# A hybrid decoder trunk: sparse-attention projections in three wide chunks with a borrowed accumulator, and a new order of the early steps

## The chip, the cores and the metric

The kernel runs on one core of one Trainium2 chip, in one launch. The metric is the device time of an execution in microseconds (us), taken as the median of several runs. Engines are called by their names in the profile: PE is TensorE's matmul side and PEld its weight loads, DVE is VectorE, ACT is ScalarE, POOL is GpSimd, SP is SyncE, on whose queue most DMAs are issued.

## The reference

Two layers of a decoder trunk, sequence 512, model width 1024, all in float32. Per layer one projection feeds four parallel branches, which are lifted, gated, summed and projected out; a SwiGLU feed-forward follows.

```python
h = rmsnorm(x, norm_mix)
(a_x, a_b, a_c, d_q, d_k, d_v, i_q, i_k, i_w,
 g_q, g_f, g_i, g_g, m_q, gate_logits) = split_cols(h @ w_in)
y_a = a_b * causal_conv3(a_c * a_x, conv_w)                        # A: gated convolution
q = partial_rope(rmsnorm(d_q ...8 heads of 64...), cos, sin)       # B: sparse attention
k = partial_rope(rmsnorm(d_k ...1 head...), cos, sin)
iq = partial_rope(i_q ...8 heads of 64...); ik = partial_rope(i_k); iw = i_w * 8 ** -0.5
y_b = dsa_attention(q, k, d_v, iq, ik, iw)   # score = sum_h relu(iq . ik / 8) * iw; the best 128 keys
                                             # of each query; softmax attention over those
y_c = ...hgrn2 gated linear recurrence of g_q, g_f, g_i, g_g...    # C
y_m = ...cross attention of m_q into 256 memory tokens, 4 heads of 128...   # M
merged = sum over n of sigmoid(gate_logits)[n] * (branches[n] @ w_lift[n])
x = x + merged @ w_out
gate, up = split(rmsnorm(x, norm_ffn) @ ffn_w_up)
x = x + (silu(gate) * up) @ ffn_w_down
```

## The kernel before

**Products in three passes.** Every large product is done in split float32: a high and a low part of each operand, and three matmuls per tile (`mm3`, lines 270 to 272). The parts of a weight chunk are made on the chip: `Chunk` loads up to 2048 columns per partition into `w_raw` (two buffers, issued on SP), then ACT writes `w_hi` (`A`, line 97) and DVE `w_lo` (line 225), 1024 columns at a time, three buffers each.

**Accumulators.** PSUM holds three buffers "mm" (`mm_ps`, for products), two "at" (`at_ps`, for attention logits and outputs) and three "tr" (`tr_ps`, for transposes and small results). A buffer comes free when the engines that read it are done, in the order in which the program asked for buffers.

**Who sets the order.** The program is recorded step by step, and a scheduler lays the instructions of each engine into a fixed order; each engine then runs its own list strictly in turn. Splits of weights and some evictions are recorded with a priority 3000 places ahead (`AHEAD`). Steps are Python generators, and a string gives the order in which they are advanced. For the early part of each layer that is `EARLY[l]`: "b" is a step of `projections` (sparse attention), "c" of `conv_branch`, "m" of `mem_branch`, "s" of `sel`, the chain of `select(1)`, `select(2)`, `select(3)`. What is left of b, c and m after the string is run out; what is left of `sel` is woven into `lift(3)`.

**The steps.**
- `projections`: five chunks of 256, 256, 200, 256 and 256 columns. For each, the four tiles of 128 tokens follow one another: `tokens` makes one accumulator (8 k x 3 matmuls, h stationary and the weights moving), and a handler works it off at once: `c_kv`, `c_iq`, `c_last` and `c_q`. Handlers copy heads out (`unit`, `twin`), norm and rotate them (`headnorm`, `rope`), and transpose them (`heads_T`, line 754; `twin`, line 776) into qS, kS, iqS and ikS.
- `mem_branch`: a head pair is projected, then four steps per pair, each a chain: logits into an at buffer (`mk`, `qg`), maximum on DVE (line 639), exponential on ACT (`mprob`), scaling on DVE (line 651), four transposes (line 653), copies to `mpt_hi` (ACT) and `mpt_lo` (DVE, line 657), output product into the other at buffer, copies to y_m. `mpt_hi` and `mpt_lo` have one buffer each. Two of the products stand in "m" steps of their own, eight attention steps in eight more.
- `select(t)`: 8 heads of index scores in at buffers (lines 685, 686), summed on DVE, then 16 rounds of `max` and `match_replace` on DVE, giving the bias of query tile t.
- `lift(n)`: gates and lift products in pairs of 128 columns, woven with `sel` (for n = 3) or with `attend` (for n = 0, followed by `values`).
- `attend(t)`: 8 heads: logits in at buffers, line 698 on DVE, exponential and scaling on ACT (`prob`), transposes (line 709), copies `pt` on ACT, products with vt (line 715). Then the HGRN stage begins with `logits`, whose results zf, zq and zg (line 880) lie in space that the attention used.
- `final`, at the very end of the kernel, already has a product that opens all four token tiles at once on three mm buffers and one at buffer, with `tokens_wide`: for each part of the weights, for each of the four tiles, all k of that part.

Of the kernel before, what the change touches and what calls it, by code (L numbers as in the profile page):

```python
# [16 lines left out]
AF = mybir.ActivationFunctionType  # L17
# [4 lines left out]
P = 128  # L22
S = 512
NT = S // P
D = 1024
KD = D // P
# [11 lines left out]
C_AX, C_AB, C_AC, C_DQ, C_DK, C_IQ, C_IK = 0, 512, 1024, 1536, 2048, 2176, 2688  # L38
# [3 lines left out]
NONC = -2.0e38  # L42
OFF = -1.0e30
AHEAD = 3000
EARLY = ["mmbcmmbmmbsccsmmcsssmsccbmb", "mmbmmbmmcbsccsmmcsssmsccbmb"]
MM_BUFS = 3
TR_BUFS = 3
AT_BUFS = 2
# [21 lines left out]
def hybrid_trunk(ctx: ExitStack, tc: tile.TileContext, x, mem, positions, norm_mix, w_in, conv_w,  # L70
# [19 lines left out]
    def A(dst, src, func, **kw):  # L90
        name = tables.get(func)
        if name is not None and name != table["set"]:
            load = act.preload_act_table_set(name)
            for u in table["users"]:
                tc.add_manual_dep(load.ins, u.name, order, reason="table set")
            table.update(set=name, load=load.ins, users=[])
        i = act.activation(dst, src, func, **kw)  # L97
        if name is not None:
            tc.add_manual_dep(i.ins, table["load"].name, order, reason="table set")
            table["users"].append(i.ins)  # L100
        return i

    def mm_ps():
        return pmm.tile([P, 512], F32, name="mm")

    def at_ps():
        return pat.tile([P, 512], F32, name="at", bufs=AT_BUFS)

    def tr_ps():
        return pat.tile([P, 512], F32, name="tr", bufs=TR_BUFS)  # L110
# [31 lines left out]
    ps = tr_ps()  # L142
# [16 lines left out]
    ps = tr_ps()  # L159
# [19 lines left out]
    gq_b, gk_b = [], []  # L179
    for l in range(DEPTH):  # L180
        a = sp.tile([P, HD], F32, name=f"gq_raw{l}")
# [5 lines left out]
        b = consts.tile([P, HD], F32, name=f"gk{l}")  # L187
# [64 lines left out]
    def tokens(w, a, t, ps, k0=0, kt=None):  # L252
        kt = w.kt if kt is None else kt
        for k in range(k0, k0 + w.kt):
            mm3(ps, pair(a, k, slice(t * P, (t + 1) * P)), w.at(k - k0), k == 0, k == kt - 1)

    def tokens_wide(ws, a, kt, pss):

        k0 = 0
        for w in ws:  # L260
            for ks, _, _ in w.parts:
                for t, ps in enumerate(pss):
                    for k in ks:
                        mm3(ps, pair(a, k0 + k, slice(t * P, (t + 1) * P)), w.at(k), k0 + k == 0, k0 + k == kt - 1)
            k0 += w.kt

    def mm3(ps, a, b, first, last):
        ah, al = a
# [105 lines left out]
    h = new_h()  # L374
# [126 lines left out]
    def mixer(l, h, norms, cm, cf):  # L501
        mix = cm.enter_context(tc.tile_pool(name="mix", bufs=1, side="right"))
        r_t, r_b = norms()
        r8_t = small(NT, name="r8_t", bufs=2)
# [171 lines left out]
        with pool_("dsa") as dp:  # L676
            qS = dp.tile([P, 8, S], F32R, name="qS")
            kS = (dp.tile([P, S], F32R, name="k_hi"), dp.tile([P, S], F32R, name="k_lo"))
            pool.memset(f(kS[1][HD:P, :]), 0.0)
            vt = dp.tile([P, NT, HD], F32, name="vt")  # L680
# [42 lines left out]
            with pool_("idx") as ip:  # L723
                iqS = ip.tile([P, 8, S], F32R, name="iqS")
                ikS = (ip.tile([P, S], F32R, name="ik_hi"), ip.tile([P, S], F32R, name="ik_lo"))
                pool.memset(f(ikS[1][HD:P, :]), 0.0)
                iw = ip.tile([P, NT, 8], F32, name="iw")

                def rope(u, heads, t):
                    v = u[:, :, 0:ROT]  # L730
                    c = cos2[:, t:t + 1, :].to_broadcast([P, heads, ROT])
                    s = sin2[:, t:t + 1, :].to_broadcast([P, heads, ROT])
                    a = ip.tile([P, 4, ROT], F32, name="rope_a", bufs=2)[:, :heads]
                    b = ip.tile([P, 4, ROT], F32, name="rope_b", bufs=2)[:, :heads]
                    dve.tensor_mul(a, v, c)
                    dve.tensor_mul(b, v, s)
                    hf = ROT // 2
                    dve.tensor_sub(v[:, :, 0:hf], a[:, :, 0:hf], b[:, :, hf:])
                    dve.tensor_add(v[:, :, hf:], a[:, :, hf:], b[:, :, 0:hf])

                def headnorm(u, heads, gain):
                    sq = ip.tile([P, 4, HD], F32, name="hn_sq", bufs=1)[:, :heads]
                    A(sq, u, AF.Square, scale=HD ** -0.5)
                    ms = small(heads)
                    dve.tensor_reduce(ms, sq, axis=AX.X, op=OP.add)
                    r = small(heads)
                    rstd_into(r, ms, small, heads)
                    dve.tensor_mul(u, u, r[:, :, None].to_broadcast([P, heads, HD]))
                    dve.tensor_mul(u, u, gain[:, None, :].to_broadcast([P, heads, HD]))

                def heads_T(dst, h0, u, heads, t):
                    ps = tr_ps()[:, :heads * HD]
                    for i in range(heads // 2):
                        pe.transpose(ps[:, i * P:(i + 1) * P], u[:, i * P:(i + 1) * P], ident)  # L754
# [12 lines left out]

                def twin(ps, t, c0, norm, dst):
                    u = ip.tile([P, 2, HD], F32, name="twin", bufs=2)
                    A(u[:, 0, :], ps[:, c0:c0 + HD], AF.Copy, scale=r_t[:, t:t + 1])  # L770
                    if norm:
                        headnorm(u[:, 0:1], 1, gk_b[l])
                    rope(u[:, 0:1], 1, t)
                    dve.tensor_copy(u[:, 1, :], u[:, 0, :])
                    ps = tr_ps()[:, :P]
                    pe.transpose(ps, u.rearrange("p a b -> p (a b)"), ident)
                    s = slice(t * P, (t + 1) * P)
                    A(dst[0][:, s], ps, AF.Copy)
                    dve.tensor_sub(dst[1][0:HD, s], ps[0:HD], f(dst[0][0:HD, s]))

                def iq_part(ps, t, c0, heads, h0):
                    u = unit(ps, t, c0, heads)
                    rope(u, heads, t)
                    heads_T(iqS, h0, u.rearrange("p a b -> p (a b)"), heads, t)

                def c_kv(ps, t):
                    A(vt[:, t, :], ps[:, 64:128], AF.Copy, scale=r_t[:, t:t + 1])
                    twin(ps, t, 0, True, kS)
                    iq_part(ps, t, 128, 2, 0)

                def c_iq(ps, t):
                    iq_part(ps, t, 0, 4, 2)

                def c_last(ps, t):
                    A(iw[:, t, :], ps[:, 192:200], AF.Copy, scale=r8_t[:, t:t + 1])
                    iq_part(ps, t, 0, 2, 6)
                    twin(ps, t, 128, False, ikS)

                def c_q(q):
                    def go(ps, t):  # L800
                        u = unit(ps, t, 0, 4)
                        headnorm(u, 4, gq_b[l])
                        rope(u, 4, t)
                        heads_T(qS, 4 * q, u.rearrange("p a b -> p (a b)"), 4, t)
                    return go

                def select(t):
                    n = (t + 1) * P
# [307 lines left out]
```

## Time and profile before

| | before |
|---|---|
| three runs | 2047.5, 2048.2, 2047.55 us |
| median | 2047.55 us |
| the profiled execution, its own time | 2047.48 us |
| its span, first to last instruction | 2045.4 us |
| mean granted TensorE clock | 0.999 |
| DMA traffic | 203.79 MB, mean 100 GB/s |

The span is 2.1 us shorter than the execution's own time, which also holds what lies around the first and the last instruction. In rows of the timeline, the first number is the start in us from the span's start, the second the duration; in tables of stretches, each engine's busy time comes with its count of instructions, then the granted clock, the DMA share and GB/s. In lists of waits the three numbers are us in total, times, and the longest. Rows of the timeline that are alike and follow one another are merged and carry their count.

### The profile page before, as it was taken

The page shows a single profiled execution, that of the slowest core. Times are in us where ns is not written, and L with a number is a line of the kernel's source. Part 1 is how long each engine was busy: PE and PEld are TensorE (multiplying, and loading weights), DVE is VectorE, ACT ScalarE, POOL GpSimd, SP SyncE. Part 2 cuts the span into 40 slices and gives each one's busy share as a digit, 9 for nine tenths or more (in the row PEclk, how much of TensorE's full clock was granted, in tenths as well). Part 3 has the DMA queues.
Part 4 walks back from the last instruction along what each step waited for, and adds up shares of the span by engine and source line. Part 5 has one row for each costly group of instructions (what it writes and reads, how often), then busy time and mean ns, then how long its engine had stood idle before and what let it go on. Part 6 is the DMA issues. An engine that isn't in the chain of part 4 may idle for free.

```text
span 2045.4 us, 26581 instructions
## 1 busy us (share of the span) xinstructions
PE 2034.5 (99%) x10348; PEld 1715.8 (84%) x10348; DVE 1269.3 (62%) x2507; ACT 1017.5 (50%) x1834; POOL 9.8 (0%) x33
## 2 busy tenths in 40 slices
PE   8999999999999999999999999999999999999999
PEld 8998988888888888888889898888888888888887
DVE  6779998547676544334457889963777754533442
ACT  7653655766665423223355456576767633322331
POOL 0000000000000000000000000000000000000000
PEclk9999999999999999999999999999999999999999
DMA  7632232223233232233243213322223322323322
GB/s 253 220 89 94 68 93 93 64 71 93 78 118 113 83 103 93 93 105 102 87 155 94 88 58 107 97 76 63 83 83 101 126 90 96 103 75 111 97 79 93
DMA packets 187709, 203.79 MB, mean 100 GB/s; under 512 B 4270, under 2 KB 176384, under 8 KB 187456
## 3 DMA queue, kind: packets, MB, share of 16 engines
q1 hardware_dynamic: 183872, 193.56, 29.8%
q10 hardware_dynamic: 3552, 8.41, 1.1%
q8 instruction: 81, 1.33, 0.3%
q14 instruction: 44, 0.36, 0.1%
q0 software_dynamic: 160, 0.13, 0.0%
HBM read 191.60 MB, written 10.49 MB: 99 GB/s over the span
## 4 chain that ended last, share of the span: by engine, by line
PE 99%; DMA 1%; DVE 0%; ACT 0%; SPq 0%; issue 0%; DVEq 0%
PE mm L270 30%; PE mm L272 30%; PE mm L271 30%; PE tr L715 1%; PE tr L709 1%; PE at L686 1%; PE at L685 1%; PE at L272 1%; PE at L270 1%; PE at L271 1%; DMA w_raw<-in_mem_w_kv_dram 1%; PE at L963 0%; PE at L937 0%; PE tr L653 0%; PE tr L754 0%; PE tr L972 0%
## 5 line engine op out<-in xcount | busy, mean ns | idle before, releaser
L270 PE MATMUL mm<-h_hi,w_hi 128*128 128x512 f32 x1664 | 653.0, 393 | 0.0
L271 PE MATMUL mm<-h_lo,w_hi 128*128 128x512 f32 x1664 | 652.1, 392 | 0.0
L272 PE MATMUL mm<-h_hi,w_lo 128*128 128x512 f32 x1664 | 650.1, 392 | 0.0
L225 DVE TENSOR_TENSOR w_lo<-w_raw,w_hi 128x1024 fp32r<-128x1024 f32 (+1 forms) x346 | 419.5, 1213 | 364.5 <-ACT w_hi L97 361.3
L97 ACT ACTIVATE w_hi<-w_raw 128x1024 fp32r<-128x1024 f32 (+1 forms) x346 | 363.4, 1051 | 460.8 <-PE mm L271 414.5
L272 PEld LDWEIGHTS mm<-h_hi,w_lo 128*128 128x128 f32 x1664 | 312.8, 188 | 64.8 <-issue 1.2
L270 PEld LDWEIGHTS mm<-h_hi,w_hi 128*128 128x128 f32 x1664 | 312.8, 188 | 64.5 <-issue 2.2
L271 PEld LDWEIGHTS mm<-h_lo,w_hi 128*128 128x128 f32 x1664 | 312.9, 188 | 63.8 <-issue 2.0
L272 PE MATMUL mm<-w_hi,h_lo 128*128 128x256 f32 (+1 forms) x448 | 128.2, 286 | 0.0
L271 PE MATMUL mm<-w_lo,h_hi 128*128 128x256 f32 (+1 forms) x448 | 127.0, 285 | 0.0
L270 PE MATMUL mm<-w_hi,h_hi 128*128 128x256 f32 (+1 forms) x448 | 127.0, 285 | 0.0
L271 PE MATMUL mm<-a_lo,w_hi 128*128 128x512 f32 x272 | 106.3, 391 | 0.0
L270 PE MATMUL mm<-a_hi,w_hi 128*128 128x512 f32 x272 | 106.0, 390 | 0.0
L272 PE MATMUL mm<-a_hi,w_lo 128*128 128x512 f32 x272 | 105.8, 391 | 0.0
L270 PE MATMUL mm<-y_hi,w_hi 128*128 128x512 f32 x256 | 101.4, 397 | 0.0
L272 PE MATMUL mm<-y_hi,w_lo 128*128 128x512 f32 x256 | 100.6, 393 | 0.0
L271 PE MATMUL mm<-y_lo,w_hi 128*128 128x512 f32 x256 | 100.3, 392 | 0.0
L272 PEld LDWEIGHTS mm<-w_hi,h_lo 128*128 128x128 f32 x448 | 85.8, 191 | 1.4 <-issue 0.8
L270 PEld LDWEIGHTS mm<-w_hi,h_hi 128*128 128x128 f32 x448 | 85.3, 191 | 1.2 <-issue 0.8
L271 PEld LDWEIGHTS mm<-w_lo,h_hi 128*128 128x128 f32 x448 | 85.6, 191 | 0.6
L97 ACT ACTIVATE a_hi<-fg 128x512 fp32r<-128x512 f32 x44 | 27.8, 633 | 109.4 <-DVE fg L1065 109.4
L97 ACT ACTIVATE prob<-prob,small 128x128 f32<-128x128 f32 (+3 forms) x128 | 69.2, 554 | 15.2 <-DVE small L698 14.6
(358 smaller groups left out, 2946.9 us busy)
## 6 DMA issues: line engine op xcount, KB each, us to landing
w_raw<-in_w_in_dram SPq DMA_DIRECT2D x72, 1024.0 KB, 5.3
w_raw<-in_ffn_w_up_dram SPq DMA_DIRECT2D x44, 1024.0 KB, 5.1
w_raw<-in_w_lift_dram SPq DMA_DIRECT2D x32, 512.0 KB, 3.5
w_raw<-in_ffn_w_down_dram SPq DMA_DIRECT2D x16, 1024.0 KB, 5.5
w_raw<-in_mem_w_kv_dram SPq DMA_DIRECT2D x8, 1024.0 KB, 5.4
w_raw<-in_w_out_dram SPq DMA_DIRECT2D x8, 1024.0 KB, 5.2
w_raw<-in_ffn_w_down_dram SPq DMA_DIRECT2D x10, 512.0 KB, 3.4
kv<-kv ACTq DMA_DIRECT2D x8, 512.0 KB, 3.2
```

Source lines behind the costliest of these rows:

```text
L97: i = act.activation(dst, src, func, **kw)
L225: dve.tensor_sub(lo, raw[:, k:e], f(hi))
L270: pe.matmul(ps, ah, bh, start=first, stop=False)
L271: pe.matmul(ps, ah, bl, start=False, stop=False)
L272: pe.matmul(ps, al, bh, start=False, stop=last)
L685: pe.matmul(ps, q[:, hh, s], k[0][:, :n], start=True, stop=False)
L686: pe.matmul(ps, q[:, hh, s], k[1][:, :n], start=False, stop=True)
L709: pe.transpose(pp[:, (2 * e + i) * P:(2 * e + i + 1) * P], probs[2 * i + e][:, b * P:(b + 1) * P], ident)
L715: pe.matmul(pv[e * HD:(e + 1) * HD, :], vt[:, b, :], pt[:, b, e * 2 * P:(e + 1) * 2 * P], start=b == 0, stop=b == t)
```

## The change

The five chunks become three: 512 columns (query heads 6 and 7, the key, the value and index heads 0 to 3), 328 (index heads 4 to 7, the index key, the index weights) and 384 (query heads 0 to 5). Each opens all four token tiles at once, on the three mm buffers and one borrowed at buffer, and runs them with `tokens_wide`; the handlers follow when all four are recorded. `chunks` cuts the loads so that each fits w_raw: 4 + 4, 6 + 2 and 4 + 4 rows of k, which are split in 4, 3 and 4 parts. `EARLY` is new and the same for both layers: three "b" near the beginning, and nearly every "m" beside a step that holds a product.

```diff
-EARLY = ["mmbcmmbmmbsccsmmcsssmsccbmb", "mmbmmbmmcbsccsmmcsssmsccbmb"]
+EARLY = ["mmbmcmbmbsmsmcsmcsmcsmcsc", "mmbmcmbmbsmsmcsmcsmcsmcsc"]
...
+    def chunks(src, n):
+
+        per = 2 * (1024 // n)
+        return [wchunk(src[k * P:min(k + per, KD) * P], min(per, KD - k), n) for k in range(0, KD, per)]
...
-                def iq_part(ps, t, c0, heads, h0):
+                def iq_part(ps, t, c0, h0):
+                    u = unit(ps, t, c0, 4)
+                    rope(u, 4, t)
+                    heads_T(iqS, h0, u.rearrange("p a b -> p (a b)"), 4, t)
+
+                def q_part(ps, t, c0, heads, h0):
                     u = unit(ps, t, c0, heads)
+                    headnorm(u, heads, gq_b[l])
                     rope(u, heads, t)
-                    heads_T(iqS, h0, u.rearrange("p a b -> p (a b)"), heads, t)
-
-                def c_kv(ps, t):
-                    A(vt[:, t, :], ps[:, 64:128], AF.Copy, scale=r_t[:, t:t + 1])
-                    twin(ps, t, 0, True, kS)
-                    iq_part(ps, t, 128, 2, 0)
-
-                def c_iq(ps, t):
-                    iq_part(ps, t, 0, 4, 2)
+                    heads_T(qS, h0, u.rearrange("p a b -> p (a b)"), heads, t)
+
+                def c_low(ps, t):
+                    A(vt[:, t, :], ps[:, 192:256], AF.Copy, scale=r_t[:, t:t + 1])
+                    twin(ps, t, 128, True, kS)
+                    iq_part(ps, t, 256, 0)
+                    q_part(ps, t, 0, 2, 6)
 
                 def c_last(ps, t):
-                    A(iw[:, t, :], ps[:, 192:200], AF.Copy, scale=r8_t[:, t:t + 1])
-                    iq_part(ps, t, 0, 2, 6)
-                    twin(ps, t, 128, False, ikS)
-
-                def c_q(q):
...
+                    A(iw[:, t, :], ps[:, 320:328], AF.Copy, scale=r8_t[:, t:t + 1])
+                    iq_part(ps, t, 0, 4)
+                    twin(ps, t, 256, False, ikS)
+
+                def c_q(ps, t):
+                    q_part(ps, t, 0, 4, 0)
+                    q_part(ps, t, 256, 2, 4)
...
-                    for c0, n, handle in ((C_DK, 256, c_kv), (C_DK + 256, 256, c_iq), (C_DK + 512, 200, c_last),
-                                          (C_DQ, 256, c_q(0)), (C_DQ + 256, 256, c_q(1))):
-                        w = wchunk(w_in[l][:, c0:c0 + n], KD, n)
-                        for t in range(NT):
-                            ps = mm_ps()[:, :n]
-                            tokens(w, h, t, ps)
+                    for c0, n, handle in ((C_DQ + 384, 512, c_low), (C_IQ + 256, 328, c_last), (C_DQ, 384, c_q)):
+                        pss = [ps[:, :n] for ps in [mm_ps() for _ in range(MM_BUFS)] + [at_ps()]]
+                        tokens_wide(chunks(w_in[l][:, c0:c0 + n], n), h, KD, pss)
+                        for t, ps in enumerate(pss):
                             handle(ps, t)
                         yield
```

In the changed file all lines from `chunks` on move: `mm3` is at 275 to 277, the transposes of the memory steps at 658, those of the attention at 714, its products at 720.

More of the change, by code (lines that the diff above doesn't have):

```diff
@@ L779, in twin @@
                     dve.tensor_sub(dst[1][0:HD, s], ps[0:HD], f(dst[0][0:HD, s]))
-                def iq_part(ps, t, c0, heads, h0):
+                def iq_part(ps, t, c0, h0):
[3 more added lines that the diff above has]
+                def q_part(ps, t, c0, heads, h0):
                     u = unit(ps, t, c0, heads)
+                    headnorm(u, heads, gq_b[l])
                     rope(u, heads, t)
-                    heads_T(iqS, h0, u.rearrange("p a b -> p (a b)"), heads, t)
-                def c_kv(ps, t):
-                    A(vt[:, t, :], ps[:, 64:128], AF.Copy, scale=r_t[:, t:t + 1])
-                    twin(ps, t, 0, True, kS)
-                    iq_part(ps, t, 128, 2, 0)
-                def c_iq(ps, t):
-                    iq_part(ps, t, 0, 4, 2)
-                def c_last(ps, t):
-                    A(iw[:, t, :], ps[:, 192:200], AF.Copy, scale=r8_t[:, t:t + 1])
-                    iq_part(ps, t, 0, 2, 6)
-                    twin(ps, t, 128, False, ikS)
-                def c_q(q):
[L800 to L805, printed above, removed]
+                    heads_T(qS, h0, u.rearrange("p a b -> p (a b)"), heads, t)
[4 more added lines that the diff above has]
+                    q_part(ps, t, 0, 2, 6)
+                def c_last(ps, t):
+                    A(iw[:, t, :], ps[:, 320:328], AF.Copy, scale=r8_t[:, t:t + 1])
[4 more added lines that the diff above has]
+                    q_part(ps, t, 256, 2, 4)
                 def select(t):
```

## The prediction

> **What bounds the kernel now.** I read the page first (here its span and engine rows), then the waits of TensorE (PE), then the timeline.
>
> ```profile
> span 2045.4 us, 26581 instructions
> PE 2034.5 (99%) x10348; PEld 1715.8 (84%) x10348; DVE 1269.3 (62%) x2507; ACT 1017.5 (50%) x1834; POOL 9.8 (0%) x33
> PE tr L160 <- DMA rows<-in_mem_k_norm_dram: 1.9, 1, 1.9
> PE mm L271 <- DVE w_lo L225: 1.3, 2, 0.8
> PE tr L144 <- DVE ones_d L118: 1.1, 1, 1.1
> PE mm L270 <- ACT w_hi L97: 1.0, 1, 1.0
> PE tr L386 <- DVE mt_lo L388: 0.8, 2, 0.6
> ```
>
> The last five rows are all that TensorE ever waited for: 6.1 us, all at the start. So there are two ways to move the time: make TensorE's work shorter (every saved ns counts in full), or make it wait (every ns counts in full too, since nothing is waited for now). The scheduler has put something long behind every dependent step. The change must be read for both.
>
> **What TensorE saves.** A matmul's duration in the rows overlaps the next one's; its price is the distance from start to start. Rows of three widths, the first and last of unbroken runs:
>
> ```profile
> 75.67 0.39 PE L271 MATMUL mm<-h_lo,w_hi 128*128 128x512 f32 x1
> 78.39 0.40 PE L270 MATMUL mm<-h_hi,w_hi 128*128 128x512 f32 x1
> ...
> 80.23 0.28 PE L270 MATMUL mm<-w_hi,h_hi 128*128 128x256 f32 x1
> 82.97 0.28 PE L272 MATMUL mm<-w_hi,h_lo 128*128 128x256 f32 x1
> ...
> 146.03 0.28 PE L271 MATMUL mm<-w_lo,h_hi 128*128 128x200 f32 x1
> 147.59 0.27 PE L270 MATMUL mm<-w_hi,h_hi 128*128 128x200 f32 x1
> ...
> 1371.60 0.34 PE L685 MATMUL at<-k_hi,qS 128*128 128x384 f32 x1
> 1371.78 0.33 PE L686 MATMUL at<-k_lo,qS 128*128 128x384 f32 x1
> ```
>
> Between the first pair lie 12 steps: 0.227 us for 512 columns. The second: 23 steps, 0.119 us for 256. The third: 14 steps, 0.111 us for 200, so 56 columns fewer save almost nothing. The last: 0.18 us for 384 columns of other operands. The straight line through 256 and 512 gives 0.149 us for 328 (no row has that width; 0.119 and 0.18 bound it) and 0.173 for 384.
>
> Per layer each chunk takes 4 token tiles x 8 k x 3 products = 96 matmuls. Before: 96 x (4 x 0.119 + 0.111) = 56.4 us. After: 96 x (0.227 + 0.149 + 0.173) = 52.7 us. Saved: 3.7 us per layer; 3.0 with 0.18 for the 384. I take 3.5, **7 us for two layers** (6 to 7.4).
>
> The Trainium skill, TensorE: Matmul & The Clock Gate, section "Wait — 56ns, not 53.3ns?", gives N / 2.4 GHz plus about 2.5 ns per warm matmul. The trace disagrees: 111 ns at 200 columns against 86, 119 at 256 against 109. By that rule 384 fewer matmuls would save 1 us, and the sum below would be 6 us higher.
>
> **What the new accumulators make TensorE wait for.** In `projections` all four token tiles are now open at once, on the three mm buffers and one of the two at buffers. The memory attention uses two at buffers per step (logits, then output), in a chain. I followed the built program's order on TensorE, layer 0, at the 328-column chunk. When its three mm accumulators are done, the fourth (at) has not begun, since it comes behind two attention steps in the at rotation, and no other mm buffer is free. What stands there is: 4 transposes of probabilities; 1 output matmul; 6 logit matmuls of the next step; 5 output matmuls; 2 transposes of that next step; 3 small transposes; its other 2; 2 small ones; 1 output matmul; only then 19 matmuls of 328. Layer 1 has the same sequence. In the program of before, the least that stands between transposes and output is about 2.1 us of matmuls, and between logits and transposes 5.8 us. One such step of before, in rows:
>
> ```profile
> 119.31 0.28 PE L272 MATMUL at<-mk,qg_lo 128*128 128x256 f32 x1
> 119.63 0.69 DVE L639 TENSOR_REDUCE small<-at 128x2 f32<-128x512 f32 x1 [1.20 <-PE at L272]
> 121.37 0.15 DVE L641 TENSOR_TENSOR small<-small,mrs 128x2 f32<-128x2 f32 x1
> 122.50 0.54 ACT L97 ACTIVATE mprob<-at,small,mrs 128x256 f32<-128x256 f32 x1
> 123.94 0.61 DVE L651 TENSOR_SCALAR mprob<-mprob,small 128x256 f32<-128x256 f32 x2
> ...
> 128.87 0.60 PE L653 MATMUL tr<-ident,mprob 128*128 128x128 f32 x4
> 129.30 0.60 PE L754 MATMUL tr<-ident,unit 128*128 128x128 f32 x4
> 129.56 0.60 ACT L97 ACTIVATE mpt_hi<-tr 128x512 fp32r<-128x512 f32 x1 [2.00 <-PE tr L653]
> 130.19 0.69 DVE L657 TENSOR_TENSOR mpt_lo<-tr,mpt_hi 128x512 fp32r<-128x512 f32 x1 [1.82 <-ACT mpt_hi L97]
> 133.19 0.28 PE L270 MATMUL at<-mpt_hi,mv 128*128 128x256 f32 x1
> ```
>
> (a) Transposes to output. The copy mpt_hi ends at 130.16, about 1.4 us after the first transpose with a hand-over; the transposes take 0.43 of it. With nothing between, TensorE waits 0.95 us. The order has that at three of the first four steps of layer 0 and at two of layer 1 (4 matmuls of 0.227 cover the first there), and once per layer with two small transposes between (0.75). Layer 0: 3 x 0.95 + 0.75 = 3.6. Layer 1: 2.65. Sum 6.3.
>
> (b) Logits to transposes. Logits end at 119.59, the first scaled half is ready at 124.25: 4.7 us, with splits of weights (w_hi, w_lo) between. Without them: 0.69 + 0.15 + (124.25 - 122.50) + hand-overs = about 2.9. Five matmuls of 0.119 cover 0.6. The wait is 2.3 to 4.1 us, once per layer. In this stretch VectorE also works off the four token tiles' norms and ropes, so I take 3.2, 6.4 for both.
>
> (c) The late tail of the sparse attention. The `select` chain and its queue on VectorE:
>
> ```profile
> 160.00:180.00 20.00, 20.00 (x96) 16.76 (x95) 19.03 (x41) 9.19 (x18) 0.20 (x2) 1.00 0.30 97
> 320.00:340.00 20.00, 20.00 (x92) 16.61 (x91) 19.25 (x35) 11.08 (x15) 0.00 (x0) 1.00 0.25 80
> 409.65 0.71 ACT L97 ACTIVATE prob<-prob,small 128x512 f32<-128x512 f32 x1
> 410.35 1.55 ACT L97 ACTIVATE pt<-tr 128x512 f32<-128x512 f32 x3
> 411.78 1.34 ACT L97 ACTIVATE prob<-prob,small 128x512 f32<-128x512 f32 x2
> 413.01 0.48 ACT L97 ACTIVATE hv<-mm,rstd_t 128x256 f32<-128x256 f32 x1
> 445.77 0.65 PE L715 MATMUL tr<-pt,vt 128*64 128x256 f32 x4
> 446.35 0.50 PE L271 MATMUL mm<-h_lo,w_hi 128*128 128x512 f32 x1
> 446.54 0.69 DVE L880 TENSOR_TENSOR zf<-mm,rstd 128x512 f32<-128x512 f32 x1 [3.75 <-PE tr L715]
> ```
>
> In the windows the fifth column is VectorE's busy time: 19 of 20 us, so `select` is held by VectorE from 160 to 340. In the new script the scoring of `select(2)` comes behind the last memory step, and in the built order VectorE reaches the first softmax of `attend` only with the last product of `lift(0)`; before, it did so with half of that lift still to come. All of `attend` then has for cover `values` (192 matmuls of 0.119) and 72 matmuls of the HGRN logits: three mm accumulators' worth, and no fourth can start, as the last row shows: the write of zf waits for the attention's last product (L715). Before, that product had 48 and 16 of these matmuls around it.
>
> After the 72, the order has only attention: 10 matmuls of 512 (2.3 us), 32 transposes of 0.11 (3.5) and 22 products at 0.29 (445.77 to 446.35 is 4 records, two to a product; 6.4): 12.2 us of TensorE. ScalarE there has 11 copies at 0.48 (410.35 to 411.78 are three), 5 exponentials at 0.70, 6 scalings at 0.61 and 2 small copies of 0.3: 13.1 us. Laid one behind the other in the engines' order, with the last scaling, transposes, copy and product in sequence (about 2.4 us of waits), the stretch lasts 15.5 us: 3.3 us of waiting per layer, 6.6 in all (0 if TensorE arrives late; 7 per layer if ScalarE does).
>
> (d) The clock. At the start of the run TensorE was idle 2.1 us in 5:
>
> ```profile
> 10.00:15.00 5.00, 2.92 (x17) 1.86 (x16) 3.87 (x15) 4.06 (x11) 0.00 (x0) 0.99 1.04 408
> 15.00:20.00 5.00, 5.00 (x32) 5.00 (x31) 2.62 (x13) 4.81 (x11) 0.00 (x0) 0.67 1.08 358
> 15.06 0.42 PE L272 MATMUL mm<-w_hi,mt_lo 128*128 128x256 f32 x1
> 18.05 0.39 PE L271 MATMUL mm<-w_lo,mt_hi 128*128 128x256 f32 x1
> ```
>
> The granted clock (third from the right) fell to 0.67, and the 14 steps of 256 columns to 18.05 took 0.214 us each: 1.3 us more than at 0.119. The stretch of (a) and (b) has 4 to 6 us of idle in some 10. I take one such drop per layer there: 2.6 us (0 to 4 drops, 0 to 5.2).
>
> The Trainium skill, same page, section "What's actually happening", says the clock halves only after a whole idle window of about 3.4 us and comes back after a busy one. By that rule (b) alone, at most 4.1 us, would rarely do it, and the sum would be 2.6 us lower; the rows above show a drop with shorter gaps.
>
> **Edits with no cost.** One more split of weights (11 parts for 10), one more head norm per token tile and six weight loads for five per layer go to ScalarE, VectorE and SP's queue. TensorE's matmuls hide them (VectorE is 62% busy, ScalarE 50%); without cover they would count among (b) and (c). The mk and mv loads are issued with their steps on SP, as before, behind other weight loads. POOL has nothing moved past it. The order behind the attention in layer 1 is that of before, instruction by instruction.
>
> **Sum.** -7 + 6.3 + 6.4 + 6.6 + 2.6 = +14.9 us. The profiled execution took 2047.48 us (span 2045.4), 0.07 under the median of the three runs, 2047.55. Forecast: 2047.5 + 14.9 = **2062.4 us**.
>
> **Rivals.**
> 1. Faster: the chains are done before TensorE reaches them, because it enters each stretch behind its modelled time. From the point at which (a) to (d) come to less than 7 us the change wins; with none of them it gives 2047.5 - 7 = 2040.5. For it: every step of before was covered. Against: the wait in (a) needs no late engine, only the copy's own 0.6 us, and it stands six times or more with nothing between. Chance 0.11.
> 2. VectorE becomes the bound: with `select(2)` begun later, the softmax starts after `lift(0)` has ended, and the whole of `attend` slides. From the start of `select(2)` to the first softmax I count about 96 us of VectorE work in the new order beside 110 us of matmuls, so it decides from 14 us of hold-ups; 8 us per layer beyond give 2047.5 + 14.9 + 16 = 2078. Chance 0.17.
> 3. The waits of one place only: (a) and (b) stand and the tail is covered, 2047.5 - 7 + 12.7 = 2053, or the other way, 2047. The tail's 3.3 us per layer is the small difference of two long sums, which speaks for it. Chance 0.13.
> 4. The change does nothing that counts, gains and waits equal: 2047.5. The build has 192 fewer matmuls per layer, so it does what it says. Chance 0.03.
> 5. The clock stays up: 2062.4 - 2.6 = 2059.8. For it: no single wait of (a) to (c) is much longer than 4 us, while at the start the idle pieces followed one another for 13 us. Chance 0.15. This is what the page's rule on the clock says.
> 6. Narrow matmuls cost by their columns only, with the save at 1 us instead of 7: 2068.4. Against it the 200-column rows, at nearly the price of 256. Chance 0.01. This is the page's rule of N / 2.4 GHz.
>
> The forecast as it stands has 0.40.
>
> **Range and chances.** Lower bounds of the waits (3 for (a), if half its places are late for other reasons; 4.6; 0; 0) less 7.4 give 0; uppers (6.3 + 8.2 + 14 + 5.2, less 6) give +28. The range 2046 to 2079 leaves out most of rival 1 and some of rival 2. This kernel's runs tell apart about 0.2%, or 4.1 us. Faster by more: 0.11; within: 0.04 (rival 4 and the edge of 3); slower: 0.85.
>
> **What would show it.** Right: TensorE's waits in the new profile list the transposes of mprob and the products with mpt_hi as waiting for VectorE and ScalarE, some 6 us per layer (between 90 and 150 us in the first); one gap of 3 to 4 us before the HGRN logits at about 450; a start-to-start distance of 0.15 at 328 columns; a clock under 1 in a window there. Wrong: no waits on TensorE beyond the first 15 us, or a first softmax that starts long after the first matmuls of `values`.

## The result, and the profile after

The changed kernel takes 2077.67 us (median of 4 runs, 2076.84 to 2078.25) against 2047.53 us for the kernel before on the same chip: ratio 1.0146, 95% interval 1.0134 to 1.0158. It is 30.1 us slower. The forecast was 2062.4 us, 14.9 us slower: the direction was right, the size half. The measured time lies inside the stated range, 2046 to 2079 us, but by luck: its own upper terms add up to +28 us, or 2075.5, and the range was drawn 3.5 us wider than that. The line numbers of the changed kernel are 5 higher than before in the places named here (`mm3` is L275 to L277, the transposes of mprob L658, those of the handlers L759 and L781). The products with the transposed probabilities stand in the rows as "at<-mpt_hi".

First the page of the change, its span and its engines:

```profile
span 2076.1 us, 25955 instructions
...
PE 2042.9 (98%) x9964; PEld 1709.0 (82%) x9964; DVE 1277.3 (62%) x2549; ACT 1028.2 (50%) x1868; POOL 9.8 (0%) x33
```

TensorE's idle time is span less busy time: 33.2 us, where it was 10.9. That is 22.3 us of new idle time. But its busy time also rose, by 8.4 us, although it has 384 matmuls fewer. Two different things happened, then, and the list of waits shows the first (waits of TensorE; us in total, times, the longest):

```profile
PE tr L759 <- ACT iqS L97: 5.6, 2, 2.8
PE tr L658 <- DVE mprob L656: 5.2, 3, 2.6
PE at L275 <- ACT mpt_hi L97: 3.6, 5, 0.7
...
PE tr L714 <- DVE y_lo L725: 1.4, 2, 0.7
...
PE tr L759 <- DVE ik_lo L784: 1.2, 2, 0.6
...
PE tr L714 <- ACT prob L97: 1.0, 2, 0.5
...
PE tr L714 <- ACT pt L97: 0.7, 2, 0.5
```

The second and third rows and the three L714 rows were forecast. The two L759 rows, transposes of the projection's own handlers, were not, and the first of them holds the longest single wait. By the row, what ends that wait is ScalarE's copy of an earlier transpose out of a tr buffer into iqS (133.78 to 134.16 us), so what TensorE lacked there was a free tr buffer and not its input. The timeline of TensorE in layer 0 shows the place (the last bracket is the idle time ahead of the row and what ended it):

```profile
130.78 0.31 PE L277 MATMUL mm<-w_hi,h_lo 128*128 128x328 f32 x1
130.93 0.27 PE L781 MATMUL tr<-ident,twin 128*128 128x128 f32 x1
131.04 0.38 PE L759 MATMUL tr<-ident,unit 128*128 128x128 f32 x2
134.21 0.44 PE L759 MATMUL tr<-ident,unit 128*128 128x128 f32 x1 [2.79 <-ACT iqS L97]
134.82 1.09 PE L658 MATMUL tr<-ident,mprob 128*128 128x128 f32 x4 [0.17 <-DVE mprob L656]
136.60 0.58 PE L275 MATMUL at<-mpt_hi,mv 128*128 128x256 f32 x1 [0.69 <-ACT mpt_hi L97]
136.98 0.41 PE L275 MATMUL at<-mk,qg_hi 128*128 128x256 f32 x1
...
139.11 0.41 PE L277 MATMUL at<-mpt_hi,mv 128*128 128x256 f32 x1
141.91 0.66 PE L658 MATMUL tr<-ident,mprob 128*128 128x128 f32 x2 [2.39 <-DVE mprob L656]
...
144.94 0.48 PE L275 MATMUL at<-w_hi,h_hi 128*128 128x328 f32 x1
```

This is the sequence that the prediction read out of the built program: three mm accumulators done at 131, then nothing but small steps until the fourth tile begins on its borrowed at buffer at 144.94. Two things stand out beside the waits. Matmuls of 256 columns are 0.21 us apart here (136.98 to 139.11, 10 steps) and not 0.12. And a pair of transposes takes 0.66 us (141.91) where the pair at 131.04 took 0.38. That is the second effect, the clock. A table of stretches; behind the comma stand the busy times of PE, PEld, DVE and ACT, and the granted clock is third from the right:

```profile
127.30:130.70 3.40, 3.40 (x25) 3.39 (x24) 2.50 (x15) 2.70 (x12) 0.00 (x0) 1.00 0.00 0
130.70:134.10 3.40, 0.72 (x6) 0.47 (x4) 3.10 (x17) 3.17 (x12) 0.00 (x0) 1.00 0.00 0
134.10:137.50 3.40, 2.43 (x9) 1.80 (x10) 3.29 (x21) 1.56 (x5) 0.00 (x0) 0.50 0.00 0
137.50:140.90 3.40, 2.02 (x10) 1.73 (x9) 2.23 (x10) 1.20 (x4) 0.00 (x0) 0.50 0.11 20
140.90:144.30 3.40, 1.79 (x8) 1.42 (x9) 1.80 (x8) 1.54 (x6) 0.00 (x0) 0.50 0.16 57
144.30:147.70 3.40, 3.40 (x14) 3.40 (x15) 2.36 (x8) 1.24 (x5) 0.00 (x0) 0.50 0.02 5
147.70:151.10 3.40, 3.40 (x26) 3.39 (x26) 2.04 (x3) 2.53 (x4) 0.00 (x0) 0.99 0.00 0
```

The clock falls to half behind a stretch in which TensorE was busy for 0.72 of 3.40 us, stays there while the next ones are busy for 2.43, 2.02 and 1.79 us, and comes back only behind the full one. In these four stretches TensorE was busy for 9.64 us; at full clock the same work takes half, so the fall costs about 4.8 us. Layer 1 has the same four stretches from 1134 us, and one more in the attention tail:

```profile
1455.10:1458.50 3.40, 2.19 (x13) 1.06 (x12) 2.11 (x7) 3.35 (x9) 0.00 (x0) 1.00 0.00 0
1458.50:1461.90 3.40, 3.14 (x15) 2.41 (x15) 0.00 (x0) 2.09 (x5) 0.79 (x2) 0.50 0.00 0
```

The second of these two was busy for 3.14 us at half clock, 1.6 us lost. So the clock costs about 2 x 4.8 + 1.6 = 11.2 us, where the prediction had 2.6.

### The profile page after: what moved, and what is told of

Read it like the earlier page. It is cut to its first block, busy times and chain, and to the rows that moved or that the text cites. A ratio compares the mean times of both kernels' runs of the same rounds, so it can differ in the third digit from the quotient of the medians.

```text
span 2076.1 us, 25955 instructions
## 1 busy us (share of the span) xinstructions
PE 2042.9 (98%) x9964; PEld 1709.0 (82%) x9964; DVE 1277.3 (62%) x2549; ACT 1028.2 (50%) x1868; POOL 9.8 (0%) x33
## 4 chain that ended last, share of the span: by engine, by line
PE 95%; ACT 2%; DVE 1%; DMA 1%; issue 0%; SPq 0%; DVEq 0%; ACTq 0%
PE mm L275 29%; PE mm L276 28%; PE mm L277 28%; PE at L275 1%; PE at L276 1%; PE at L277 1%; PE tr L720 1%; PE tr L714 1%; PE at L691 1%; PE at L690 1%; ACT prob L97 1%; DMA w_raw<-in_mem_w_kv_dram 1%; PE at L940 0%; PE at L966 0%; PE tr L975 0%; PE tr L625 0%
## 5 line engine op out<-in xcount | busy, mean ns | idle before, releaser
L275 PE MATMUL mm<-h_hi,w_hi 128*128 128x512 f32 x1664 | 651.9, 393 | 0.7 <-DVE gate L581 0.7
L277 PE MATMUL mm<-h_hi,w_lo 128*128 128x512 f32 x1664 | 649.2, 391 | 0.0
L225 DVE TENSOR_TENSOR w_lo<-w_raw,w_hi 128x1024 fp32r<-128x1024 f32 (+2 forms) x348 | 420.0, 1208 | 359.0 <-ACT w_hi L97 349.9
L97 ACT ACTIVATE w_hi<-w_raw 128x1024 fp32r<-128x1024 f32 (+2 forms) x348 | 364.0, 1047 | 475.4 <-PE mm L276 423.7
L275 PEld LDWEIGHTS mm<-h_hi,w_hi 128*128 128x128 f32 x1664 | 312.6, 188 | 66.7 <-issue 2.2
L277 PEld LDWEIGHTS mm<-h_hi,w_lo 128*128 128x128 f32 x1664 | 312.6, 188 | 65.3 <-issue 1.0
L275 PE MATMUL mm<-a_hi,w_hi 128*128 128x512 f32 x272 | 105.9, 389 | 0.0
L277 PE MATMUL mm<-a_hi,w_lo 128*128 128x512 f32 x272 | 105.6, 390 | 0.0
L277 PE MATMUL mm<-y_hi,w_lo 128*128 128x512 f32 x256 | 100.5, 393 | 0.0
L275 PE MATMUL mm<-y_hi,w_hi 128*128 128x512 f32 x256 | 99.4, 394 | 0.9 <-ACT w_hi L97 0.9
L277 PE MATMUL mm<-w_hi,h_lo 128*128 128x256 f32 (+3 forms) x272 | 87.0, 320 | 0.0
L276 PE MATMUL mm<-w_lo,h_hi 128*128 128x256 f32 (+3 forms) x272 | 86.9, 320 | 0.0
L275 PE MATMUL mm<-w_hi,h_hi 128*128 128x256 f32 (+3 forms) x272 | 84.3, 320 | 0.0
L97 ACT ACTIVATE gate_e<-gate 128x512 f32<-128x512 f32 x64 | 40.3, 630 | 67.7 <-DVE gate L524 67.0
L524 DVE TENSOR_TENSOR gate<-mm,rstd 128x512 f32<-128x512 f32 x64 | 44.0, 687 | 30.2 <-PE mm L277 29.9
L1063 DVE TENSOR_TENSOR fg<-mm,rstd 128x512 f32<-128x512 f32 x44 | 30.2, 691 | 52.1 <-PE mm L277 52.1
```

What stands on the lines that cost most here:

```text
L225: dve.tensor_sub(lo, raw[:, k:e], f(hi))
L275: pe.matmul(ps, ah, bh, start=first, stop=False)
L276: pe.matmul(ps, ah, bl, start=False, stop=False)
L277: pe.matmul(ps, al, bh, start=False, stop=last)
L524: dve.tensor_mul(g, ps, r_b)
L1063: dve.tensor_mul(dst, ps, r_b)
```

## The experiments

Theory A: the wide chunks are the cause. All four tiles end within a few matmuls of each other; their handlers fall on VectorE and ScalarE together; no accumulator is free meanwhile, so TensorE is left with chains of small steps. That makes it idle (22 us), and so sparsely busy that the clock falls (11 us). Rivals: the new order string makes the waits (B); the borrowed at buffer does, because it shares a rotation with the memory steps (C); the clock falls for another reason than the waits (E).

**The old order string with the wide chunks, and the new one with the old chunks.**

The first run, e1, is the change with the string of before:

```diff
-EARLY = ["mmbmcmbmbsmsmcsmcsmcsmcsc", "mmbmcmbmbsmsmcsmcsmcsmcsc"]
+EARLY = ["mmbcmmbmmbsccsmmcsssmsccbmb", "mmbmmbmmcbsccsmmcsssmsccbmb"]
```

The second, e2, is the kernel before with the same line the other way round.

> The three wide chunks with the borrowed accumulator stay; the order string of the early steps goes back to that of before. Theory A (the wide chunks make the waits: all four token tiles end together, their handlers occupy VectorE and ScalarE, and no accumulator is free meanwhile; the order string only decides where this lands): TensorE still waits some 5 to 12 us per layer in the memory steps, the clock still falls there, and the attention tail at 450 us, which has its cover back in this order, loses its 1.8 us per layer: 2060 to 2077 us. Theory B (the new order string makes the waits): the waits are gone and the 7 us of saved matmuls show: 2040 to 2047 us.

> The five chunks of before, token tile by token tile on the three mm accumulators, with the order string of the change alone. Theory A (wide chunks): single token tiles end every 2.7 to 5 us and their handlers are spread, so each memory step keeps a product beside it; within 3 us of before, 2045 to 2051 us, with no fall of the clock after 15 us. Theory B (order string): the waits of the change without its 7 us of savings, 2075 to 2085 us.

Measured: 2093.39 us (ratio 1.0223, 1.0208 to 1.0238) and 2048.77 us (1.0004, 0.9995 to 1.0014). The second was as theory A has it; the string by itself is free. The first missed both ranges: with the wide chunks the old string is worse by 16 us than the new one. The longest entry of its list of waits, and then two stretches:

```profile
PE tr L658 <- DVE mprob L656: 13.1, 6, 4.1
```

```profile
280.70:284.10 3.40, 0.00 (x0) 0.00 (x0) 3.23 (x11) 1.20 (x4) 0.00 (x0) 1.00 0.01 2
284.10:287.60 3.50, 2.68 (x9) 2.12 (x10) 3.40 (x10) 0.66 (x2) 0.00 (x0) 0.51 0.00 0
```

A memory step now stands alone at 280 us too, with VectorE full (the third busy time): a whole stretch without a matmul, and half clock behind it. From 440 to 470 us this run has no wait at all (0.5 us are left in layer 1), and e2, with the new string and the old chunks, has none in the tail either: the tail's waits take the new string and the wide chunks together. The early waits come with either string. B falls.

**A fourth mm accumulator in place of the borrowed one.**

```diff
-MM_BUFS = 3
-TR_BUFS = 3
+MM_BUFS = 4
+TR_BUFS = 2
-pss = [ps[:, :n] for ps in [mm_ps() for _ in range(MM_BUFS)] + [at_ps()]]
+pss = [mm_ps()[:, :n] for _ in range(MM_BUFS)]
```

The product in `final`, which also borrowed an at buffer, takes its four from mm in the same way.

> The change with a fourth mm accumulator in place of the borrowed one (and one buffer less for transposes), so that the memory steps and the chunks no longer share a rotation. Theory A (the handlers of a chunk end together and hold all four accumulators): the wait moves, since the next chunk can't begin its fourth tile before the handlers of the chunk ahead are done; TensorE still waits 5 to 12 us per layer there: 2065 to 2080 us. Theory C (the borrowed at buffer in the rotation of the memory steps makes the waits): 2041 to 2052 us.

Measured: 2084.47 us (1.0173, 1.0156 to 1.0190; four runs from 2081.42 to 2088.82, the profile is that of the slowest). That is above the ranges of both theories. The waits of TensorE:

```profile
PE tr L658 <- DVE mprob L656: 5.9, 4, 2.3
PE at L275 <- ACT mpt_hi L97: 4.9, 6, 1.1
...
PE tr L714 <- ACT pt L97: 3.6, 6, 0.7
PE mm L275 <- ACT twin L97: 3.1, 4, 1.2
```

The handler waits on L759 have become waits of the next chunk for an accumulator that a handler still reads (mm <- twin), as theory A says; the memory steps wait as before. But the run also has waits of its own: 3.6 us of L714 <- pt in the tail, where the change has 0.7, which the missing transpose buffer may have made, and one of 4.4 us (mm <- ku) near 67 us, ahead of the wide chunks. So it excludes C as the whole cause but does not price it.

**Useless work in the waits.** If the clock falls because TensorE is sparsely busy, more work should keep it up.

```diff
+FILL = {(0, 0, 0): 4, (0, 0, 1): 20, (0, 1, 0): 14, (0, 1, 1): 4}
-                        py = at_ps()[:, :2 * P]
+                        fill = at_ps()
+                        for _ in range(FILL.get((q, j, hf), 0)):
+                            pe.matmul(fill, h[0][:, 0, 0:P], h[0][:, 0, :], start=True, stop=True)
+                        py = fill[:, :2 * P]
```

> The change with 42 more matmuls of 512 columns per layer, of no use, into the accumulator of four memory steps just ahead of their output products, where TensorE waits (about 0.227 us each, 9.5 us per layer, 19 us in all if nothing hides them). Theory D (the clock fell because the waits left TensorE sparsely busy): the clock in 130 to 148 us stays at 0.9 or more, which saves up to 6.8 us per layer, and the added matmuls lie mostly in the waits: 2062 to 2077 us, less than the change itself although work is added. Rival E (the clock falls there for another cause, or the handlers and not the waits set the time): it still shows 0.5 there, and the time is 2078 to 2097 us.

Measured: 2076.26 us (2075.67 to 2076.87; ratio 1.0138, 1.0123 to 1.0153): no slower than the change, with 84 matmuls of 0.227 us more, 19.1 us of work. Its page:

```profile
span 2073.9 us, 26124 instructions
...
PE 2053.8 (99%) x10048; PEld 1718.8 (83%) x10048; DVE 1276.1 (62%) x2549; ACT 1027.6 (50%) x1868; POOL 9.8 (0%) x33
```

The same place of layer 0 in stretches:

```profile
132.40:135.80 3.40, 3.40 (x18) 2.77 (x17) 3.33 (x20) 2.18 (x8) 0.00 (x0) 1.00 0.00 0
135.80:139.20 3.40, 2.57 (x19) 2.21 (x17) 3.21 (x18) 2.04 (x6) 0.00 (x0) 1.00 0.00 0
139.20:142.60 3.40, 2.38 (x13) 1.97 (x13) 2.37 (x9) 1.58 (x5) 0.00 (x0) 1.00 0.09 27
142.60:146.00 3.40, 3.40 (x23) 3.04 (x22) 0.65 (x3) 1.09 (x4) 0.00 (x0) 1.00 0.16 55
```

No stretch here is busy for less than 2.38 us, and the clock stays at 1.00. The page gives the price: idle time fell from 33.2 to 20.1 us, by 13.1; busy time rose by 10.9 us and not by 19.1. The missing 8.2 us are the clock's. One stretch in layer 1 still fell (busy for 3.41 us, so 1.7 lost), and the start of the run has one slow stretch more than that of the change (busy for 2.8, 1.4 lost); with these the clock's price in the change is 11.3 us, close to the 11.2 worked out above from its own stretches. E falls: the clock fell because the waits left TensorE sparsely busy.

**Less work for VectorE.** In the change VectorE is nearly full where the waits are (its busy time is the third behind the comma):

```profile
120.00:130.00 10.00, 10.00 (x70) 9.97 (x69) 8.82 (x45) 6.57 (x26) 0.00 (x0) 1.00 0.48 157
130.00:140.00 10.00, 5.88 (x28) 4.71 (x26) 8.55 (x44) 5.69 (x20) 0.00 (x0) 0.71 0.00 0
```

One run, e5, leaves the rotation out, the other, e6, moves it to POOL:

```diff
                 def rope(u, heads, t):
+                    return
```

```diff
-                    dve.tensor_mul(a, v, c)
-                    dve.tensor_mul(b, v, s)
+                    pool.tensor_mul(a, v, c)
+                    pool.tensor_mul(b, v, s)
...
-                    dve.tensor_sub(v[:, :, 0:hf], a[:, :, 0:hf], b[:, :, hf:])
-                    dve.tensor_add(v[:, :, hf:], a[:, :, hf:], b[:, :, 0:hf])
+                    pool.tensor_sub(v[:, :, 0:hf], a[:, :, 0:hf], b[:, :, hf:])
+                    pool.tensor_add(v[:, :, hf:], a[:, :, hf:], b[:, :, 0:hf])
```

> The change without the rotation of the heads in the handlers (the four VectorE operations per unit at L740 to L744 are left out, so queries and keys are not rotated). In the trace of the change VectorE has no gap of note from 117 to 140 us and these operations are about 12.6 of its 36 us there. Theory F (VectorE's backlog is what the dependent steps wait for): TensorE's waits at 130 to 148 us fall from 6.6 us to 3 or less, and the clock falls for at most one window there; 2055 to 2067 us. Rival G (the order on TensorE alone makes the waits, each step's own chain being longer than what stands before it): waits and clock as in the change, 2072 to 2079 us.

> The change with the same rotation done on GpSimd (POOL) in place of VectorE; POOL is idle in this stretch. Theory F (VectorE's backlog): the time falls too, if POOL's own chain of four operations is not the slower one: 2057 to 2072 us. Rival G (order on TensorE alone): 2075 to 2085 us, more than the change where POOL's operations take longer than VectorE's.

Measured: 2067.14 us without the rotation (1.0095, 1.0078 to 1.0112), 2072.93 us with it on POOL (1.0123, 1.0108 to 1.0138). The page of the first, and two stretches of it:

```profile
span 2064.9 us, 25736 instructions
...
PE 2036.3 (99%) x9964; PEld 1705.4 (83%) x9964; DVE 1254.0 (61%) x2325; ACT 1027.3 (50%) x1868; POOL 9.8 (0%) x33
```

```profile
130.00:140.00 10.00, 5.88 (x34) 5.12 (x33) 6.28 (x21) 6.25 (x23) 0.00 (x0) 0.83 0.08 27
140.00:150.00 10.00, 9.09 (x54) 8.85 (x53) 6.40 (x14) 6.57 (x17) 0.00 (x0) 0.83 0.08 19
```

The numbers fit neither theory as a whole: the first time is 0.1 us over theory F's range, the second lies between the two ranges. Without the rotation, idle time fell by 4.6 us (28.6 against 33.2), far from all of it: TensorE still idles 5.0 us from 130 to 150, against the 3 that theory F allowed. Of the 11.2 us by which the span shrank, the other 6.6 are busy time with the same matmuls, most of it the clock's: with somewhat shorter gaps the first slow stretch (134.6 to 138.0) is busy for 2.93 us, and the clock is back behind it, though it falls once more, behind a stretch busy for 0.95 us, where theory F allowed one fall. Two rows of TensorE's waits say what did not change:

```profile
PE tr L658 <- DVE mprob L656: 5.7, 4, 2.3
PE at L275 <- ACT mpt_hi L97: 4.9, 5, 1.3
```

The memory steps wait as long as in the change or longer (10.6 us against 8.8), while the wait on iqS, 5.6 us, is gone. So VectorE's backlog is part of the cause, through the handlers and the clock. The waits of the memory steps remain with VectorE two thirds busy; the order on TensorE, as the prediction had it, is what is left to explain them, but no run shows that by itself. ScalarE was as full as VectorE where the longest wait stands (3.17 us of 3.40 from 130.70), and no run took work off ScalarE. On POOL the same operations give less, and TensorE then waits for them (the list has 4.4 us of L759 for POOL's rows).

**Narrow chunks, all four tiles at once.**

```diff
-                        w = wchunk(w_in[l][:, c0:c0 + n], KD, n)
-                        for t in range(NT):
-                            ps = mm_ps()[:, :n]
-                            tokens(w, h, t, ps)
+                        pss = [ps[:, :n] for ps in [mm_ps() for _ in range(MM_BUFS)] + [at_ps()]]
+                        tokens_wide([wchunk(w_in[l][:, c0:c0 + n], KD, n)], h, KD, pss)
+                        for t, ps in enumerate(pss):
                             handle(ps, t)
```

> The five narrow chunks of before and the new order string, but in each chunk all four token tiles at once, with the borrowed accumulator, and their handlers at its end. Against the run with the same string and tile after tile (2048.8 us). Theory H (opening all four tiles at once is the cost, whatever the width): waits of 3 to 10 us per layer, 2055 to 2075 us. Rival K (the width: fewer, longer chunks press the same handlers into less TensorE work; narrow bunches are cleared in time): 2046 to 2054 us.

Measured: 2064.30 us (1.0082, 1.0067 to 1.0097), 15.5 us over the same string with tile after tile, within theory H's range, so opening all tiles at once costs by itself. Idle time is 17.2 us, 6.1 more than with tile after tile. The new string has only three "b", so the last two of five chunks run behind it, here from 213 to 249 us beside `select`, and that is where the clock falls, with TensorE busy for 2.18 us:

```profile
231.10:234.50 3.40, 2.18 (x10) 1.20 (x8) 3.23 (x9) 2.36 (x6) 0.00 (x0) 1.00 0.00 0
234.50:238.00 3.50, 2.40 (x9) 1.43 (x9) 3.30 (x8) 1.90 (x5) 0.00 (x0) 0.51 0.02 5
```

**Four chunks, tile after tile, and the same four at once.** Three weight buffers hold a whole chunk of up to 341 columns, so wider chunks can also be worked tile after tile. The heads are regrouped so that four slices of w_in follow each other without a gap:

```diff
+for c0, n, handle in ((C_DK + 64, 320, c_v), (C_IQ + 256, 328, c_last),
+                      (C_DQ + 256, 320, c_qk), (C_DQ, 256, c_q)):
+    ws = chunks(w_in[l][:, c0:c0 + n], n)
 e8, e9:
+    for t in range(NT):
+        ps = mm_ps()[:, :n]
+        k0 = 0
+        for w in ws:
+            tokens(w, h, t, ps, k0, KD)
+            k0 += w.kt
+        handle(ps, t)
 e10:
+    pss = [ps[:, :n] for ps in [mm_ps() for _ in range(MM_BUFS)] + [at_ps()]]
+    tokens_wide(ws, h, KD, pss)
+    for t, ps in enumerate(pss):
+        handle(ps, t)
```

e8 and e10 have the new order string; e9 has "mmbcmmbmmbsccsmmcsssmsccbm" in both layers.

> The new order string with four chunks of 320, 328, 320 and 256 columns (values and four indexer heads; the other four with their key and weights; four query heads with the key; four query heads), worked tile after tile on the three mm accumulators as before, nothing borrowed. By start-to-start distances 96 x (2 x 0.147 + 0.150 + 0.119) = 54.0 us per layer, 2.4 us less than before. Theory H (opening all four tiles at once, and not the width, is the cost): no waits of note beyond the start, 2041 to 2048 us. Rival K (wider chunks press the handlers together however they are worked): waits and a fallen clock at 110 to 150 us, 2050 to 2066 us. A third outcome: the three weight buffers are all held until a chunk's last tile, and the next chunk waits for its split weights, 1 to 2 us at each of four chunks, 2048 to 2060 us with waits of mm for w_hi and w_lo.

> The same four chunks, tile after tile, with the order string that layer 0 has before, in both layers (its last two of five product steps now find four chunks). Theory H: 2041 to 2047 us, faster than before if the weights come in time. Rival K: 2050 to 2066 us. With the weights late, 2048 to 2060 us. If this one and the one with the new string agree within 3 us, the order string doesn't matter once the tiles are worked one after the other.

> The same four chunks of 320, 328, 320 and 256 columns, the same order string and handlers as the run with four chunks and the new string (2042.2 us), but in each chunk all four token tiles at once, on three mm accumulators and a borrowed one, with the handlers at its end: this one thing apart. Theory H (opening all four tiles at once is the cost): waits of TensorE of 3 to 8 us per layer and one or more clock falls, 2053 to 2075 us. Rival K (the widths, or the change's own three chunks, are the cost): 2040 to 2047 us.

Measured: e8 2042.24 us (0.9972, 0.9961 to 0.9983), e9 2045.67 us (0.9988, 0.9980 to 0.9997), e10 2050.60 us (1.0013, 1.0004 to 1.0023). e8 is faster than both kernels, 5.8 us under before; 4.8 us of it (2 x 2.4) were worked out from its 192 fewer matmuls. Its page:

```profile
span 2040.0 us, 26156 instructions
...
PE 2028.4 (99%) x10156; PEld 1710.2 (84%) x10156; DVE 1266.4 (62%) x2461; ACT 1017.7 (50%) x1812; POOL 9.8 (0%) x33
```

From 30 us to the end, the list of TensorE's waits has one row:

```profile
PE tr L714 <- ACT pt L97: 0.9, 2, 0.5
```

So the four chunks don't wait for late weights, and no handler or memory step is waited for. The old string gave 3.4 us more than the new one, a little over the 3 set as its limit, so the string matters slightly here too; 2.4 us of it stand in one row of e9's list, products of `lift` that wait for a gate (L524).

e10 differs from e8 in the one point of theory H and costs 8.4 us more. That is above rival K's range and below H's own. It has no fall of the clock behind the start, 2.5 us more idle time (14.1 against 11.6) and 5.8 us more busy time (2034.2 against 2028.4); one more slow stretch at the start (busy for 2.0 us) accounts for 1.0 us of the busy time, and the rest stays open. Its waits are others than the change's:

```profile
PE mm L275 <- ACT w_hi L97: 3.8, 5, 1.1
PE at L275 <- ACT mpt_hi L97: 1.3, 3, 0.4
```

TensorE waits for split weights and a little for a memory step, never for a handler's transpose. Opening all tiles at once thus cost time with five chunks (15.5 us) and with four (8.4 us), but not by one mechanism, and the cost doesn't simply grow as the chunks get fewer. The rest of the change's 30 us needs its three chunks too, which no run works tile after tile. But e10 differs from the change in one more thing: the string's three "b" take all three chunks of the change early (the last ends at 171 us), while e10's fourth chunk runs at 222 to 260 us. The change therefore has more of the handlers' work in the early place. What part of the difference is the larger bunch of handlers, what part their place, and what part the order on TensorE that follows, no run here separates.

## Why the prediction was half right

- **TensorE's savings, 7 us: right.** In the new trace 22 steps of 328 columns without a break take 3.28 us, 0.149 each, and 11 of 384 take 1.91 us, 0.174 each, against the 0.149 and 0.173 of the prediction; 3.6 us per layer. Rival 6 falls.

```profile
123.01 0.31 PE L275 MATMUL mm<-w_hi,h_hi 128*128 128x328 f32 x1
...
126.29 0.31 PE L276 MATMUL mm<-w_lo,h_hi 128*128 128x328 f32 x1
...
151.89 0.34 PE L276 MATMUL mm<-w_lo,h_hi 128*128 128x384 f32 x1
...
153.80 0.33 PE L277 MATMUL mm<-w_hi,h_lo 128*128 128x384 f32 x1
```

- **(a) transposes to output, 6.3 us: place right, size too large.** 3.6 us in five waits of at most 0.7 (at<-mpt_hi), where the forecast had seven, five of them at 0.95.
- **(b) logits to transposes, 6.4 us: right.** 5.2 us; 2.39 and up to 2.6 us, once per layer, at the step that was named.
- **(c) the attention tail, 6.6 us: place right, size half.** 3.1 us in the three L714 rows. The sum of two long chains was put at 3.3 us per layer; it is 1.5 to 1.7. And it is not the one gap of 3 to 4 us that was to show it, but three of 0.3 to 0.7 us per layer among the attention's transposes.
- **Not foreseen: the handlers' own transposes.** 5.6 and 1.2 us on L759. The prediction counted these transposes as cover for (a) and (b) and gave them no chain of their own; they hang on ScalarE and VectorE like the memory steps. By chance they fill what (a), (b) and (c) lack: 19.3 us of waits were forecast, and idle time grew by 22.3, the rest of it in small rows.
- **(d) the clock, 2.6 us: this is the step that failed.** It was taken as one drop of one stretch per layer, sized by the start of the run, where a full stretch of work brings the clock back at once. Here four stretches stay at half in each layer, 4.8 us, and one more in the tail: about 11 us, more than twice its upper bound of 5.2. What was missed is how the clock comes back: in these runs TensorE was busy for nearly a whole stretch first (2.7 us or more of 3.4), and a place with waits of 0.6 to 2.8 us in a row doesn't deliver that. Rival 5, with the clock staying up, went the wrong way.
- **The sum with measured terms:** -7.2 + 22.3 + 11.2 = 26.3 us of the 30.7 by which the span grew. The other 4.4 us are busy time. An estimate puts them on the waits too: a matmul with another close behind it costs 0.15 us at 328 columns or 0.12 at 256, but the last one before a wait is busy for its whole 0.31 or 0.28, 0.16 more. The lists have 33 waits in the change and 7 before, and 26 x 0.16 = 4.2 us. No run tests this. Of the 15.8 us that the forecast of the growth lacked, 8.6 are thus the clock's, 3.0 the idle time's and 4.4 these.
- **Rival 2, VectorE as the bound,** gave the nearest time, 2078, by the wrong place: the first softmax (L703) starts at 390.1 us, ahead of the first result of `values` at 392.8, and the tail's waits are short. But VectorE's backlog was there, some 250 us earlier, among the handlers; without the rotation the time falls by 10.5 us, mostly through the clock.

## What to carry to other kernels

An accumulator that holds out longer for a wider product also brings its readers together: count what else the engine can do from the last matmul of the bunch to the first free accumulator. Where a change leaves TensorE waiting, price the wait twice: once as idle time, once as the work around it at half clock until a nearly full stretch of work follows. Part of the saving in matmuls could be had here without opening all tiles: four chunks worked tile after tile gave 5.8 us where three chunks at once lost 30.

## What the runs showed of the hardware

The granted clock was 1.0 or 0.5 and changed in steps of 3.4 us: it stayed at half for 3.4, 6.8, 10.2, 13.7 or 17.1 us. Over all kernels here, behind the first 15 us of each, every stretch of 3.4 us at full clock with TensorE busy for at most 1.6 us was followed by half clock (0.00 in e1, 0.72 in the change, 1.57 in e4), none busy for over 2.2 us was (2.24 in e9 and 2.32 in e1 were not), and between these both happened (2.18 in e7 was, 2.20 in e5 was not). At half clock, stretches busy for 2.9 us or more brought full speed back (2.93 in e5), those under 2.6 did not (2.43 in the change), and between these both happened. Busy times here rest on modelled ends of the matmuls. The Trainium skill, TensorE: Matmul & The Clock Gate, section "What's actually happening", has the same two states, half and full, and the same 3.4 us, but the clock falling after an idle window. The trace disagrees on that: the clock fell behind stretches with 0.72 and 2.19 us of matmuls.
